# Twenty-eight transposes of the identity ahead of the first matmul of a two-layer encoder trunk

## The chip, the cores and the metric

The kernel runs on one core of one Trainium2 chip. The metric is the device time of one execution in microseconds, taken as the median of several runs; lower is better.

## What is computed

Two pre-norm residual layers over 256 tokens of width 2048, all in fp32. Layer 0 mixes tokens with bidirectional retention beside 2-D neighbourhood attention, layer 1 with differential attention; each layer then attends to 256 memory tokens and ends in a SwiGLU feed-forward of hidden width 5632.

```python
for i in range(DEPTH):                                   # DEPTH = 2
    h = rms_norm(x, norm_mix_g[i])
    if i % 2 == 0:
        x = x + retention_na_mixer(h, w_in_ab[j], ...)   # one projection: h @ w_in_ab, 2048 x 7168
    else:
        x = x + diff_attention_mixer(h, w_in_c[j], ...)
    m = rms_norm(mem, norm_mem_g[i])
    x = x + memory_cross_attention(rms_norm(x, norm_xattn_g[i]), m, ...)
    x = x + swiglu_ffn(rms_norm(x, norm_ffn_g[i]), w_ffn_in[i], w_ffn_out[i])
return x
```

## The kernel before

Nearly all of the work is large matrix products, and all of them go through one function, `gemm`. A weight matrix is cut into blocks of 512 rows by 512 columns (1 MB, tile `raw`), and each block into two units of 256 rows. `prepare` (lines 269 to 296) fetches a block with one DMA on SP's queue (line 282; the very first block comes in two halves, lines 278 and 280, with a tile of the transposed input between them) and splits each unit in two parts for accuracy: ScalarE rounds it to `wh` (line 292), and VectorE takes the remainder `wl` (line 293). Three `raw` buffers, three of `wh` and three of `wl` rotate. `gemm` calls `prepare` so that three units are ready or under way before TensorE takes one.

A unit is 12 matmuls of 128x128 by 512 columns: for each of two token halves and two row tiles, `wh` with the high part of the activations (line 321), `wl` with the high part (322), `wh` with the low part (323). So the first matmul of a unit needs `wh`, and the second needs `wl`. For the order of the first projection (list `start`, lines 245 and 246), `raw` block 0 feeds units 0 and 1, block 1 units 2 and 3, block 2 units 4 and 5, and so on; with three buffers, the DMA of block 4 (units 8 and 9) takes the buffer of block 1, and can be issued when `wl` of unit 3 has been written.

The activations come into the first projection ready transposed from DRAM (tiles `xt`, line 127), are multiplied by the gain and split into `hTh` on ScalarE (350) and `hTl` on VectorE (351). Between these lie small jobs that `Side` hands out unit by unit: the parameters, the retention decays (from line 169, a chain of small VectorE operations on tile `pl`), the lambdas, and the neighbourhood bias, whose tables come by four DMAs on POOL's queue (line 577). Every engine executes its instructions in the order in which the program issues them.

`ident`, the 128x128 identity, is made on GpSimd near the top (`make_identity`, lines 130 and 131). In the kernel before, TensorE first uses it in `turn` (line 345), where four 128x128 transposes go to one PSUM tile `pt` of the pool `ps_t`, which has two buffers. The first such call comes some way into the first projection.

Of the kernel before, what the change touches and what calls it, by code (L numbers as in the profile page):

```python
# [10 lines left out]
F32 = mybir.dt.float32  # L11
# [5 lines left out]
P = 128  # L17
D = 2048
T = 256
# [62 lines left out]
def trunk_kernel(  # L82
# [8 lines left out]
    nc = tc.nc  # L91

    def pool(name, bufs, **kw):
        return ctx.enter_context(tc.tile_pool(name=name, bufs=bufs, **kw))
# [16 lines left out]
    ps_t = pool("ps_t", 2, space=bass.MemoryType.PSUM)  # L111
# [17 lines left out]
    load_xt(0)  # L129
    ident = const.tile([P, P], F32, name="ident")  # L130
    make_identity(nc, ident)
    mhalf = const.tile([P, 16], F32, name="mhalf")
    nc.gpsimd.memset(mhalf, -0.5)
    warm = const.tile([P, 1], F32, name="warm")
# [112 lines left out]
    for layer in range(2):  # L247
        j = layer // 2
# [510 lines left out]
    for layer in range(2):  # L759
        j = layer // 2  # L760
# [150 lines left out]
```

## Time and profile before

| | us |
|---|---|
| median of 3 runs | 2475.66 |
| lowest, highest | 2475.55, 2479.15 |
| the profiled execution | 2475.84 |
| its span, first to last instruction | 2474.1 |

The profile is of one execution. It gives the busy time of each engine over the span, the chain of work that ended last, and a timeline of single instructions with the idle time ahead of each and what ended it. A matmul's listed duration includes its way through the array, and matmuls overlap; their pace is read from the distance of their starts. The granted clock of TensorE is 1.00 in every row of this profile.

### The profile page before, as it was taken

The page shows a single profiled execution, that of the slowest core. Times are in us where ns is not written, and L with a number is a line of the kernel's source. Part 1 is how long each engine was busy: PE and PEld are TensorE (multiplying, and loading weights), DVE is VectorE, ACT ScalarE, POOL GpSimd, SP SyncE. Part 2 cuts the span into 40 slices and gives each one's busy share as a digit, 9 for nine tenths or more (in the row PEclk, how much of TensorE's full clock was granted, in tenths as well). Part 3 has the DMA queues.
Part 4 walks back from the last instruction along what each step waited for, and adds up shares of the span by engine and source line. Part 5 has one row for each costly group of instructions (what it writes and reads, how often), then busy time and mean ns, then how long its engine had stood idle before and what let it go on. Part 6 is the DMA issues. An engine that isn't in the chain of part 4 may idle for free.

```text
span 2474.1 us, 28641 instructions
## 1 busy us (share of the span) xinstructions
PE 2456.3 (99%) x11184; PEld 2037.1 (82%) x11184; DVE 1475.7 (60%) x1833; ACT 1187.0 (48%) x1538; POOL 138.2 (6%) x215
## 2 busy tenths in 40 slices
PE   8999999999999999999999999999999999999999
PEld 6888888888888888888888888888888888888887
DVE  6775565675655555555567766767655545555554
ACT  6554464564443444444455555655544444443443
POOL 1000001010000000000010000010100000000000
PEclk9999999999999999999999999999999999999999
DMA  8555567656765666566674555675766656665665
GB/s 288 177 169 179 175 226 245 214 192 213 233 216 200 205 212 225 194 198 226 225 241 164 170 170 168 212 249 171 237 222 210 215 188 214 228 206 200 207 217 175
DMA packets 250184, 511.82 MB, mean 207 GB/s; under 512 B 11328, under 2 KB 11968, under 8 KB 250048
## 3 DMA queue, kind: packets, MB, share of 16 engines
q1 hardware_dynamic: 239568, 484.47, 58.5%
q0 software_dynamic: 8320, 23.08, 4.1%
q10 hardware_dynamic: 2160, 2.44, 0.3%
q8 instruction: 87, 1.43, 0.2%
q14 instruction: 49, 0.40, 0.0%
HBM read 486.88 MB, written 23.07 MB: 206 GB/s over the span
## 4 chain that ended last, share of the span: by engine, by line
PE 92%; DMA 3%; DVE 3%; ACT 1%; POOL 1%; issue 0%; ACTq 0%; SPq 0%; POOLq 0%; DVEq 0%
PE acc L322 30%; PE acc L321 30%; PE acc L323 30%; DMA zz<-zd 2%; DVE wl L293 1%; DMA zd<-zz 1%; PE pt L345 1%; ACT wh L292 0%; PE pt L545 0%; PE pa_s L437 0%; PE pa_s L436 0%; DVE x_sb L741 0%; PE pa_s L435 0%; POOL zz L394 0%; PE pa_r L595 0%
## 5 line engine op out<-in xcount | busy, mean ns | idle before, releaser
L293 DVE TENSOR_TENSOR wl<-raw,wh 128x1024 fp32r<-128x1024 f32 (+1 forms) x865 | 1053.7, 1221 | 870.8 <-ACT wh L292 870.4
L292 ACT CAST wh<-raw 128x1024 fp32r<-128x1024 f32 (+1 forms) x865 | 909.1, 1051 | 1158.2 <-PE acc L323 1132.8
L322 PE MATMUL acc<-wl,hTfh 128*128 128x512 f32 x1408 | 547.9, 389 | 0.6 <-DVE wl L293 0.6
L323 PE MATMUL acc<-wh,hTfl 128*128 128x512 f32 x1408 | 547.7, 389 | 0.0
L321 PE MATMUL acc<-wh,hTfh 128*128 128x512 f32 x1408 | 547.7, 389 | 0.0
L321 PE MATMUL acc<-wh,hTh 128*128 128x512 f32 x832 | 332.0, 399 | 9.8 <-ACT wh L292 8.3
L322 PE MATMUL acc<-wl,hTh 128*128 128x512 f32 x832 | 325.7, 391 | 0.9 <-DVE wl L293 0.9
L323 PE MATMUL acc<-wh,hTl 128*128 128x512 f32 x832 | 325.8, 392 | 0.0
L322 PEld LDWEIGHTS acc<-wl,hTfh 128*128 128x128 f32 x1408 | 264.3, 188 | 56.2 <-DVE wl L293 1.4
L323 PEld LDWEIGHTS acc<-wh,hTfl 128*128 128x128 f32 x1408 | 264.3, 188 | 54.9
L321 PEld LDWEIGHTS acc<-wh,hTfh 128*128 128x128 f32 x1408 | 264.3, 188 | 54.9
L322 PE MATMUL acc<-wl,aTh 128*128 128x512 f32 x704 | 274.0, 389 | 0.2 <-DVE wl L293 0.2
L323 PE MATMUL acc<-wh,aTl 128*128 128x512 f32 x704 | 273.9, 389 | 0.0
L321 PE MATMUL acc<-wh,aTh 128*128 128x512 f32 x704 | 273.9, 389 | 0.0
L321 PEld LDWEIGHTS acc<-wh,hTh 128*128 128x128 f32 x832 | 157.2, 189 | 40.0 <-ACT wh L292 8.3
L323 PEld LDWEIGHTS acc<-wh,hTl 128*128 128x128 f32 x832 | 156.7, 188 | 34.0
L322 PEld LDWEIGHTS acc<-wl,hTh 128*128 128x128 f32 x832 | 157.2, 189 | 31.2 <-DVE wl L293 1.8
L394 POOL DMA_DIRECT2D zz<-zd x160 | 87.3, 552 | 1589.9 <-DMA zd<-zz 1410.9
L322 PEld LDWEIGHTS acc<-wl,aTh 128*128 128x128 f32 x704 | 132.1, 188 | 28.2 <-DVE wl L293 0.8
L321 PEld LDWEIGHTS acc<-wh,aTh 128*128 128x128 f32 x704 | 132.1, 188 | 27.5
L323 PEld LDWEIGHTS acc<-wh,aTl 128*128 128x128 f32 x704 | 132.1, 188 | 27.3
L321 PE MATMUL acc<-wh,oTh 128*128 128x512 f32 x256 | 100.2, 392 | 0.0
(189 smaller groups left out, 1940.3 us busy)
## 6 DMA issues: line engine op xcount, KB each, us to landing
raw<-in_w_ffn_in SPq DMA_DIRECT2D x176, 1024.0 KB, 5.1
raw<-in_w_ffn_out SPq DMA_DIRECT2D x88, 1024.0 KB, 5.1
raw<-in_w_in_ab SPq DMA_DIRECT2D x55, 1024.0 KB, 5.2
raw<-in_w_in_c SPq DMA_DIRECT2D x48, 1024.0 KB, 5.2
zd<-zz SPq DMA_DIRECT2D x40, 512.0 KB, 3.8
zz<-zd POOLq DMA_DIRECT2D x160, 128.0 KB, 5.4
raw<-in_w_out_ab SPq DMA_DIRECT2D x16, 1024.0 KB, 5.1
raw<-in_w_xkv SPq DMA_DIRECT2D x16, 1024.0 KB, 5.0
```

Of the source, the lines that this page charges most:

```text
L292: nc.scalar.copy(wh[:, js], raw[:, rs])
L293: nc.vector.tensor_sub(wl[:, js], raw[:, rs], wh[:, js])
L321: nc.tensor.matmul(acc[t], lhsT=hi[:, kt, ts], rhs=wh[:, j], start=first and j == 0, stop=False)
L322: nc.tensor.matmul(acc[t], lhsT=hi[:, kt, ts], rhs=wl[:, j], start=False, stop=False)
L323: nc.tensor.matmul(acc[t], lhsT=lo[:, kt, ts], rhs=wh[:, j], start=False, stop=last and j == 1)
L345: nc.tensor.transpose(pt[:, j, t * P:(t + 1) * P], srcs[t][:, c:c + P], ident)
L394: nc.gpsimd.dma_start(zT[32 * j:32 * j + 32].rearrange("a (i n) -> a i n", i=4), zd[:, :, j].rearrange("i a n -> a i n"))
```

## The change

Right after the identity is made, TensorE transposes it 28 times: seven tiles named `idle` are taken in turn from the pool `ps_t` under the tag `pt`, and each gets four transposes of `ident`, laid out as in `turn`. Nothing reads these tiles. Nothing else is changed.

```diff
     load_xt(0)
     ident = const.tile([P, P], F32, name="ident")
     make_identity(nc, ident)
+
+    for _ in range(7):
+        idle = ps_t.tile([P, 2, T], F32, tag="pt", name="idle")
+        for j in range(2):
+            for t in range(2):
+                nc.tensor.transpose(idle[:, j, t * P:(t + 1) * P], ident, ident)
     mhalf = const.tile([P, 16], F32, name="mhalf")
```

## Rows read from the trace of the kernel before

**Rows 1.** The page: span, and busy time of each engine with its share.

```profile
span 2474.1 us, 28641 instructions
PE 2456.3 (99%) x11184; PEld 2037.1 (82%) x11184; DVE 1475.7 (60%) x1833; ACT 1187.0 (48%) x1538; POOL 138.2 (6%) x215
```

**Rows 2.** The page: the chain that ended last, shares by engine.

```profile
PE 92%; DMA 3%; DVE 3%; ACT 1%; POOL 1%; issue 0%; ACTq 0%; SPq 0%; POOLq 0%; DVEq 0%
```

**Rows 3.** TensorE's waits, 0 to 200 us: total, times, longest.

```profile
PE acc L321 <- ACT wh L292: 8.3, 1, 8.3
PE pa_o L436 <- DVE pl L430: 1.6, 1, 1.6
...
```

**Rows 4.** Timeline of TensorE: start, duration, instruction, idle before it and its releaser.

```profile
8.28 0.80 PE L321 MATMUL acc<-wh,hTh 128*128 128x512 f32 x1 [8.28 <-ACT wh L292]
9.49 0.80 PE L322 MATMUL acc<-wl,hTh 128*128 128x512 f32 x1 [0.42 <-DVE wl L293]
10.08 0.63 PE L323 MATMUL acc<-wh,hTl 128*128 128x512 f32 x1
...
13.92 0.56 PE L323 MATMUL acc<-wh,hTl 128*128 128x512 f32 x1
14.32 0.39 PE L321 MATMUL acc<-wh,hTh 128*128 128x512 f32 x1
14.54 0.39 PE L322 MATMUL acc<-wl,hTh 128*128 128x512 f32 x1
...
33.36 0.40 PE L321 MATMUL acc<-wh,hTh 128*128 128x512 f32 x1
33.59 0.40 PE L322 MATMUL acc<-wl,hTh 128*128 128x512 f32 x1
...
97.97 0.40 PE L321 MATMUL acc<-wh,hTh 128*128 128x512 f32 x1
98.20 0.40 PE L322 MATMUL acc<-wl,hTh 128*128 128x512 f32 x1
```

**Rows 5.** Timeline of VectorE: the remainders wl of units 0 to 6 and 8.

```profile
8.74 1.29 DVE L293 TENSOR_TENSOR wl<-raw,wh 128x512 fp32r<-128x512 f32 x2
...
11.54 1.22 DVE L293 TENSOR_TENSOR wl<-raw,wh 128x1024 fp32r<-128x1024 f32 x1
...
15.07 2.35 DVE L293 TENSOR_TENSOR wl<-raw,wh 128x1024 fp32r<-128x1024 f32 x2
...
20.04 2.36 DVE L293 TENSOR_TENSOR wl<-raw,wh 128x1024 fp32r<-128x1024 f32 x2
23.76 1.22 DVE L293 TENSOR_TENSOR wl<-raw,wh 128x1024 fp32r<-128x1024 f32 x1 [1.37 <-ACT wh L292]
...
32.10 1.22 DVE L293 TENSOR_TENSOR wl<-raw,wh 128x1024 fp32r<-128x1024 f32 x1 [1.23 <-ACT wh L292]
```

**Rows 6.** Timeline of ScalarE: wh of units 3 and 8.

```profile
14.52 1.05 ACT L292 CAST wh<-raw 128x1024 fp32r<-128x1024 f32 x1 [0.83 <-DVE pl L187]
...
31.01 1.05 ACT L292 CAST wh<-raw 128x1024 fp32r<-128x1024 f32 x1 [3.35 <-DMA raw<-in_w_in_ab]
```

**Rows 7.** Timelines of SP (block 4 issued) and POOL (identity made, bias tables issued).

```profile
17.45 0.38 SPq L282 DMA_DIRECT2D raw<-in_w_in_ab  x1
...
1.57 0.28 POOL masks.py:199 TENSOR_SCALAR_AFFINE_SELECT ident<-ident 128x128 f32<-128x128 f32 x1
...
16.71 2.62 POOL L577 DMA_DIRECT2D bias<-in_na_rpb  x4 [0.37 <-POOL bias L572]
```

**Rows 8.** Stretches: length, busy time by engine, granted clock, DMA share, GB/s.

```profile
8.00:20.00 12.00, 11.31 (x38) 8.79 (x39) 10.74 (x35) 7.51 (x14) 2.82 (x5) 1.00 1.04 391
20.00:28.00 8.00, 8.00 (x37) 6.64 (x36) 5.53 (x7) 6.08 (x11) 0.00 (x0) 1.00 1.05 242
28.00:46.00 18.00, 18.00 (x81) 14.89 (x80) 12.60 (x18) 11.93 (x21) 0.00 (x0) 1.00 1.03 373
```

**Rows 9.** Timeline of TensorE: six transposes in a row, later in the kernel.

```profile
530.47 0.82 PE L345 MATMUL pt<-ident,x_sb 128*128 128x128 f32 x6
```

## The prediction, made before the change was run

> **What bounds the kernel now.** I read the page first. TensorE is busy for 99% of the span [rows 1] and makes up 92% of the chain that ended last [rows 2], so time saved elsewhere is worth nothing, and a matmul that starts earlier is worth something only if no later supply makes TensorE wait again. Next I read TensorE's waits [rows 3]: the longest is the one at the start, 8.3 us until the first weights have landed and been rounded. The change works inside that wait. Its own first matmuls stand in the timeline of TensorE [rows 4]. The first starts at 8.28, the second waits for `wl` until 9.49, and from 10.08 to 13.92 ten matmuls start over nine equal steps: (13.92 - 10.08) / 9 = 0.427 us. From 14.32 on the steps are shorter: from 14.32 to 33.36 lie seven units of 12, so (33.36 - 14.32) / 84 = 0.227 us. 512 columns in 0.427 us are 1.2 GHz, the lower level of the clock; 0.227 us belongs to the upper one. The granted clock reads 1.00 in the stretch of 8 to 20 us as in the others [rows 8], so that column does not show the difference here, and I go by the pace. Before the pace rose at 14.32, TensorE had been idle up to 8.28 and had then done one unit.
>
> **The prize, if all of it arrives.** At the upper level from the second matmul on, unit 0 ends its issue at 9.49 + 11 x 0.227 = 11.99 instead of 14.32 [rows 4]. That is 2.33 us, and the largest gain that the early clock can give, since from 14.32 on the pace is the upper one already.
>
> **The transposes themselves.** They need only the identity, done at 1.57 + 0.28 = 1.85 [rows 7]; I let them start at 2.0. Later in the kernel six transposes in a row take 0.82 us [rows 9], and one alone 0.27 of that, so the step is about (0.82 - 0.27) / 5 = 0.11 us. That is at the upper level. No row shows transposes at the lower one. Lower bound: 0.11 us each, 3.1 us for 28, done at 5.1. My value is 0.11 times the ratio of the matmul's two paces, 0.427 / 0.227 = 1.88: 0.207 us each, 5.8 us, done at 7.8, which is 0.5 us before the first matmul. Upper bound: no faster than the 512-column matmul at the lower level, 0.427 us each, 12.0 us, done at 14.0. I take the middle value because the transpose has a row of its own and only the clock is scaled. TensorE is the only engine that gets new instructions; no queue of SP, ScalarE or POOL is passed, and no DMA is added. Queued behind them on TensorE is the first matmul alone. The second cannot start before 9.49 anyway, so the cover is 28 transposes ending by about 9.1, and beyond that each late microsecond delays unit 0. The two buffers of `ps_t` are taken over within the seven tiles without a reader, so no other engine is waited for; if each of the five take-overs drained the array, that would be 5 x 0.27 = 1.4 us more and an end at 9.2, still about inside the cover. Below nothing this cannot go. The next user of those buffers comes tens of microseconds later.
>
> **Where the 2.33 us go.** Now I follow units 1 to 8 with the new start and the old supply. That supply doesn't follow TensorE. VectorE works from 8.74 to 22.40 on remainders, low parts of activations and the chain of decays; its pieces of that stretch [rows 5] have no idle time before them that TensorE ended. So the `wl` times stand as they are:
>
> - Unit 1 could begin at 11.99, but its `wl` is done at 11.54 + 1.22 = 12.76. Its second matmul goes then instead of at 12.22: a stall of about 0.6 us, and unit 2 begins at 12.8 + 11 x 0.227 = 15.3.
> - Unit 2: `wl` done at the middle of the pair, 15.07 + 2.35 / 2 = 16.25. Stall of 0.7 to 0.8 us; unit 3 begins at 18.8 instead of 19.76.
> - Units 3 to 7: `wl` of unit 3 is done at 17.42, of units 4 and 5 by 22.40, before they are wanted, so unit 8 would begin at 18.8 + 5 x 2.72 = 32.4 instead of 33.36. ScalarE gets back the `wh` buffers sooner, so that units 6 and 7 are no later than before relative to TensorE.
> - Unit 8: its `wh` started at 31.01 after 3.35 us of waiting for the DMA [rows 6], and its `wl` is done at 32.10 + 1.22 = 33.32 [rows 5]. Before, its second matmul went at 33.59 [rows 4]. That is a margin of 0.27 us, and this margin is all that can be gained as long as the block's landing doesn't move.
>
> Does the landing move? The block's DMA was issued at 17.45 [rows 7], just after the remainder of unit 3 freed the buffer at 17.42 [rows 5], and that is in VectorE's unmoved stretch. From then to its landing the DMA engines are full: share 1.04 to 1.05 in the rows from 8 to 28 us, and 1.03 after [rows 8]. What can be issued earlier are the bias tables at 16.71 [rows 7]. ScalarE rounds unit 3 at 14.52 [rows 6]; the page puts the 0.83 us before it down to a `pl` that it does not read, and I take it for the wait for unit 0's `wh` buffer, which unit 0's last matmul, begun at 13.92 [rows 4], gives back. At most 0.83 us of that would be gained for the gains behind it and for the tables. But they share the same full engines and landed ahead of block 4 before as well, so the bytes in front of block 4 are the same. I cost that at nothing; bounds are 0.8 us earlier or later at unit 8.
>
> So 2.33 - 0.6 - 0.75 - 0.77 = 0.21 us are left, which agrees with the margin of 0.27 less a handover of some 0.06 us from `wl` to the matmul (8.74 plus a little over half of 1.29 against 9.49 [rows 4, 5] puts that at up to 0.1). Behind unit 8 the chain is mostly TensorE's, and its other waits end on work that TensorE itself released, so 0.2 us reach the end. The longest of these idle times, 1.6 us [rows 3], did not bring the slow pace back: at 97.97 and 98.20 the step is 0.23 [rows 4]. So the pause between the last transpose and 9.49, about as long at 0.207 us each, should not either, though there the transposes stand in the place of matmuls.
>
> **The sum.** The profiled execution is 2475.84 = 2474.1 of span and 1.7 around it. With 0.2 less it is 2475.6. The median is 0.2 below the profiled execution, so the forecast for the median is 2475.66 - 0.2 = 2475.5.
>
> **The rivals.**
>
> 1. The change doesn't do what it says: the pace stays at 0.427 us until 14.3 because the transposes don't lift the clock. Nothing in the trace shows a stretch of transposes by themselves, so no row decides it. The transposes end at 7.8, in the cover, and the time is that of before: 2475.7. The Trainium skill has this as a rule, in "TensorE: Matmul & The Clock Gate", Part 4: PE-mode transpose: the upper level is said not to engage for transposes, since they do not count as TensorE's work in the same way. By that rule this change gives nothing; no run shown here tests it.
> 2. The weights come sooner too: block 4 lands earlier by what the early clock moves ahead of it. With the 0.8 us of the bound above it is 2475.5 - 0.8 = 2474.7; if no later block binds either, the full gain, 2475.66 - 2.33 = 2473.3. Against it speaks the full DMA [rows 8].
> 3. Slower: the transposes run past the cover. The place is the second matmul at 9.49. If the clock does not rise, it decides from (9.49 - 2.0) / 28 = 0.27 us for each; at the upper bound of 0.427 they end at 14.0, unit 0 is 14.0 - 9.5 = 4.5 us late, and the time is 2480.1. If the clock has risen by the end of them, the stalls above absorb 2.1 us first, it decides from (9.49 + 2.33 - 2.0) / 28 = 0.35 us, and at 14.0 the loss is 4.5 - 2.3 = 2.2 us: 2477.8. Against it: the rows of transposes put 0.207 us well below both points.
>
> **How the numbers follow.** The forecast has a chance of 0.54, rival 1 of 0.30, rival 2 of 0.07, rival 3 of 0.09. They differ by little: 2475.5, 2475.7, 2473.3 to 2474.7, 2477.8 to 2480.1. A measurement of this kernel can tell about 0.2% from no change, which is 5 us here. The largest possible gain is 2.33 us, under half of that; rival 3 reaches 4.5 us at its worst. So faster has 0.02 and slower 0.03, for what I have not seen, and no change has 0.95. The range goes from the full gain, 2473.3, to the mild end of rival 3, 2477.8, and leaves out the worst of it; the three runs of before lie within 2475.55 to 2479.15, so a single run can be above.
>
> **What would show it.** In the profile after: transposes of `ident` from about 2.0, step near 0.2 us, ended before 8.28. For the forecast, steps of 0.227 us right behind 9.49, and three new waits of line 322 for `wl`, near 12.2, 15.5 and 32.6, of 0.6, 0.75 and 0.8 us; unit 8's second matmul near 33.4, and all later work 0.2 us early. Steps of 0.427 up to about 14.3 would be rival 1. A first or second matmul later than 9.49 would be rival 3. A `wh` of unit 8 that starts well before 31.0 would be rival 2. I would be wrong altogether if the end moved by more than 2.4 us down or 4.5 up.

## The result, and the profile after

| | before | after |
|---|---|---|
| median, both in one comparison | 2476.60 us | 2479.81 us |
| lowest, highest | 2474.20, 2480.47 | 2477.86, 2483.92 |
| the profiled execution, its span | 2475.84, 2474.1 | 2481.13, 2479.4 |

The ratio after to before is 1.0014, with a 95% interval of 1.0007 to 1.0020: 1.7 to 5.0 us slower, 3.2 us between the medians. The forecast was 0.2 us faster, with a range that ended at 2477.8.

The page after, against [rows 1, 2]: TensorE is busy 3.1 us longer, and its share of the chain rises from 92 to 94%.

```profile
span 2479.4 us, 28696 instructions
PE 2459.4 (99%) x11212; PEld 2040.8 (82%) x11212; DVE 1476.1 (60%) x1833; ACT 1187.0 (48%) x1538; POOL 138.5 (6%) x215
...
PE 94%; DVE 2%; DMA 2%; ACT 0%; POOL 0%; issue 0%; ACTq 0%; SPq 0%; DVEq 0%; POOLq 0%
```

The timeline of TensorE, against [rows 4] (all lines of the kernel are six higher than before, so 327, 328 and 329 are the three matmul lines):

```profile
8.29 0.79 PE L327 MATMUL acc<-wh,hTh 128*128 128x512 f32 x1 [8.29 <-ACT wh L298]
...
11.81 0.63 PE L327 MATMUL acc<-wh,hTh 128*128 128x512 f32 x1
12.24 4.14 PE L137 MATMUL idle<-ident 128*128 128x128 f32 x28
16.13 0.48 PE L328 MATMUL acc<-wl,hTh 128*128 128x512 f32 x1
...
17.37 0.40 PE L327 MATMUL acc<-wh,hTh 128*128 128x512 f32 x1
```

This one view overthrows the premise of the forecast. The first 8.29 us of TensorE are as empty as before. The 28 transposes stand at 12.24, behind the seventh matmul of unit 0, in the middle of the work that they were to precede. They hold TensorE for 16.13 - 12.24 = 3.89 us. The five matmuls behind them then take 17.37 - 16.13 = 1.24 us instead of 14.32 - 12.24 = 2.08, since the pace rose while the transposes ran. So unit 1 starts at 17.37 instead of 14.32: 3.89 - 0.84 = 3.05 us late.

The place is no accident of the execution: the program has them there as built. An engine runs its instructions in the order of the built program, and the build does not keep the order of the source. On ScalarE the built order over the opening changed as well, and VectorE's remainders follow it; SP's and POOL's did not:

```
before:  wh 1, 2, 3 | hTh 4 to 7 | wh 4, 5 | ... | wh 6 | hTh 8 | wh 7 | hTh 9 to 11 | wh 8
after:   wh 1, 2 | hTh 4 to 7 | wh 3, 4 | ... | wh 5 | hTh 8 to 10 | wh 6 | hTh 11 | wh 7
```

(the number behind `wh` is the unit, the one behind `hTh` the row tile of the activations). ScalarE's timeline before has, behind `wh` of unit 3 [rows 6], these lines:

```profile
15.47 1.71 ACT L350 ACTIVATE hTh<-xt,gcol 128x256 fp32r<-128x256 f32 x4
...
23.63 0.51 ACT L350 ACTIVATE hTh<-xt,gcol 128x256 fp32r<-128x256 f32 x1
25.40 1.05 ACT L292 CAST wh<-raw 128x1024 fp32r<-128x1024 f32 x1 [1.26 <-PE acc L323]
26.35 1.31 ACT L350 ACTIVATE hTh<-xt,gcol 128x256 fp32r<-128x256 f32 x3
```

In ScalarE's timeline after, the changed order has a price of its own: three `hTh` wait for a tile of transposed input until 27.15, and `wh` of unit 6 stands behind them.

```profile
12.68 1.04 ACT L298 CAST wh<-raw 128x1024 fp32r<-128x1024 f32 x1 [1.66 <-DMA raw<-in_w_in_ab]
13.63 1.70 ACT L356 ACTIVATE hTh<-xt,gcol 128x256 fp32r<-128x256 f32 x4
17.57 1.05 ACT L298 CAST wh<-raw 128x1024 fp32r<-128x1024 f32 x1 [2.24 <-PE acc L329]
...
27.15 1.31 ACT L356 ACTIVATE hTh<-xt,gcol 128x256 fp32r<-128x256 f32 x3 [3.07 <-DMA xt<-in_x_t]
28.36 1.04 ACT L298 CAST wh<-raw 128x1024 fp32r<-128x1024 f32 x1
```

So there are two suspects: the place of the transposes on TensorE, and the new order on the other engines. Of the 3.05 us, 0.9 come back where TensorE waited 1.6 us before [rows 3]; its wait there is 0.7 after:

```profile
PE pa_o L442 <- DVE pl L436: 0.7, 1, 0.7
```

Followed matmul by matmul, this profile is behind that wait between 1.5 and 2.7 us late up to 1600 us. The rest of the 5.3 us between the two spans arises between 1600 and 1900 us, in waits of this execution (3.4 us there against 0.8 before); a second profile of the changed kernel ends 2.5 us above the span of before.

### The profile page after: what moved, and what is told of

Read it like the earlier page. It is cut to its first block, busy times and chain, and to the rows that moved or that the text cites. A ratio compares the mean times of both kernels' runs of the same rounds, so it can differ in the third digit from the quotient of the medians.

```text
span 2479.4 us, 28696 instructions
## 1 busy us (share of the span) xinstructions
PE 2459.4 (99%) x11212; PEld 2040.8 (82%) x11212; DVE 1476.1 (60%) x1833; ACT 1187.0 (48%) x1538; POOL 138.5 (6%) x215
## 4 chain that ended last, share of the span: by engine, by line
PE 94%; DVE 2%; DMA 2%; ACT 0%; POOL 0%; issue 0%; ACTq 0%; SPq 0%; DVEq 0%; POOLq 0%
PE acc L328 30%; PE acc L327 30%; PE acc L329 30%; DMA zz<-zd 1%; PE pt L351 1%; DVE wl L299 1%; DMA zd<-zz 0%; PE pt L551 0%; PE pa_s L443 0%; PE pa_s L442 0%; PE pa_s L441 0%; PE pa_r L601 0%; ACT wh L298 0%; DVE x_sb L747 0%; DMA lrow<-in_lambda_k 0%
## 5 line engine op out<-in xcount | busy, mean ns | idle before, releaser
L328 PEld LDWEIGHTS acc<-wl,aTh 128*128 128x128 f32 x704 | 132.2, 188 | 27.5
```

The lines of the kernel that those rows point to most:

```text
L328: nc.tensor.matmul(acc[t], lhsT=hi[:, kt, ts], rhs=wl[:, j], start=False, stop=False)
```

## The experiments

**Is it the length of what stands between the matmuls?** One tile of transposes instead of seven, and fourteen:

```diff
-    for _ in range(7):
+    for _ in range(1):      # few4;  range(14) in many56
```

> The change with one tile instead of seven: 4 transposes, which stand in the built order at the same place, after the seventh matmul of unit 0. Theory A (place and length): 4 steps of 0.213 us push unit 0's last five matmuls back by 0.85 us, some of it given back because the pace rises at about 14.3 as before; unit 1 starts near 14.8 instead of 14.32, and the time is 2476.6 to 2477.1 us. Theory B (the order on the other engines, changed by the mere presence of transposes, costs the 3 us): 2479 to 2480 us.

> The change with fourteen tiles instead of seven: 56 transposes after the seventh matmul of unit 0. Theory A (length on the path): the added 28 run at the upper pace, 0.11 us each, so 3.1 us more than the changed kernel: unit 1 starts near 20.4 instead of 17.37, and the time is about 2482.9 us. Theory B (one-off disturbance): 2479.8 us as with 28.

few4: 1.0002 [0.9993, 1.0011], medians 2475.30 against 2475.20. many56: 1.0026 [1.0016, 1.0035], 2482.18 against 2475.20, 7.0 us. TensorE's timelines, few4 first, then many56:

```profile
12.08 0.60 PE L137 MATMUL idle<-ident 128*128 128x128 f32 x4
...
13.68 0.39 PE L327 MATMUL acc<-wh,hTh 128*128 128x512 f32 x1
```

```profile
12.29 7.04 PE L137 MATMUL idle<-ident 128*128 128x128 f32 x56
...
20.33 0.39 PE L327 MATMUL acc<-wh,hTh 128*128 128x512 f32 x1
```

With 56, unit 1 starts at 20.33, 2.96 us behind the changed kernel: 28 more at 0.11 us. So the length counts, but many56 is not a clean test of it: its ScalarE, VectorE and SP stand in a further changed order, and by unit 9 short delays have made the 2.96 us 3.6. Its 7.0 us are 3.8 more than the changed kernel's 3.2, and the intervals are about 2 us either way. With four, unit 1 even starts early (13.68), because the pace rose sooner in that execution; and few4's built order is nearly that of before, so it clears neither suspect.

**The transposes where the words put them.** The matmuls of the first units get an edge, an ordering that the build has to keep, which puts them behind the last transpose:

```diff
+                    if at["phase"] == 1 and b < 2 and u < 2:
+                        tc.add_manual_dep(head.ins, last_idle.ins.name, ...NoSync..., reason="idle first")
```

> The same 28 transposes, but the matmuls of the first units carry an edge that puts them behind the last transpose in TensorE's order; nothing else is edited. Theory A (place): the change cost time only because the built program has the transposes after the seventh matmul of unit 0, at 12.24 us. Then here they run from about 2.0 to 8 us at steps of 0.21 us or less, nothing of them is on the path, and the time is that of before or up to 1 us less: 2475.6 to 2476.6 us against 2476.6. If transposes alone lift the clock, the steps behind 9.5 us are 0.227 us, else 0.427 us up to about 14.3; the time tells these two apart by 0.2 us at most, the timeline does. Theory B (count): 28 transposes ahead of or inside the opening cost their 3 us wherever they stand, or disturb the order of the other engines by as much: 2479.8 us as in the changed kernel.

> 56 transposes with the edge that puts them ahead of the first matmul. If transposes alone lift the clock, their step falls from 0.21 to 0.11 us within the row, they end between 9 and 12 us, and the stalls for wl that the prediction reckoned (2.1 us in all) take up the lateness: the time is within 0.5 us of before, 2476.1 to 2477.1 us. If they don't lift it, they run at 0.21 us to the end, 2.0 + 56 x 0.21 = 13.8 us, unit 0 is 4.3 us late and the time is up to 2481 us.

Both missed by far: early28 1.0036 [1.0023, 1.0048], 2484.65 against 2475.20; early56 1.0046 [1.0034, 1.0059], 2486.79. The timeline of TensorE in early28 (331 and 332 are the second and third matmul lines), then its stretches (length, busy time and count by engine, granted clock, DMA share, GB/s):

```profile
1.91 4.72 PE L137 MATMUL idle<-ident 128*128 128x128 f32 x28 [1.91 <-POOL ident masks.py:199]
8.48 0.50 PE L327 MATMUL acc<-wh,hTh 128*128 128x512 f32 x1 [1.84 <-ACT wh L298]
9.83 0.51 PE L331 MATMUL acc<-wl,hTh 128*128 128x512 f32 x1 [0.85 <-DVE wl L299]
10.17 0.40 PE L332 MATMUL acc<-wh,hTl 128*128 128x512 f32 x1
...
29.84 0.79 PE L327 MATMUL acc<-wh,hTh 128*128 128x512 f32 x1 [3.81 <-ACT wh L298]
31.16 0.79 PE L331 MATMUL acc<-wl,hTh 128*128 128x512 f32 x1 [0.53 <-DVE wl L299]
```

```profile
2.00:4.00 2.00, 2.00 (x10) 2.00 (x11) 0.00 (x0) 0.68 (x2) 0.89 (x4) 1.00 0.81 237
4.00:6.00 2.00, 2.00 (x16) 2.00 (x15) 1.25 (x6) 0.91 (x2) 0.00 (x0) 1.00 0.54 168
...
32.00:34.00 2.00, 2.00 (x6) 1.52 (x6) 1.84 (x3) 1.05 (x3) 0.00 (x0) 0.50 0.80 212
```

The opening is what the forecast wanted: the transposes start at 1.91, the count per 2 us rises from 10 to 16 while nothing but transposes runs, and from 10.17 the matmuls step at 0.23 us. Unit 1 starts 1.83 us early, at 12.49. Then it is lost: at unit 5 TensorE idles 3.81 us for a `wh`, the granted clock falls to 0.50, and the twelve matmuls of the unit run at the slow pace. ScalarE's timeline names the cause, the one seen in the changed kernel, now one unit earlier: `wh` of unit 5 stands behind three `hTh` whose input lands at 27.5.

```profile
27.54 1.31 ACT L359 ACTIVATE hTh<-xt,gcol 128x256 fp32r<-128x256 f32 x3 [6.72 <-DMA xt<-in_x_t]
28.76 1.03 ACT L298 CAST wh<-raw 128x1024 fp32r<-128x1024 f32 x1
```

The edge had rearranged the other engines further. In early56 it is VectorE's order: in unit 3 TensorE waits 8.94 us for a `wl` that stands behind a `bias`, whose table lands near 28.4 us. A first try to mend the order kept only the `hTh` and `hTl` behind the `wh` and `wl` of before:

```diff
+AFTER = {4: 3, 5: 3, 6: 3, 7: 3, 8: 6, 9: 7, 10: 7, 11: 7, 12: 10, ...}   # row tile: unit
...
+            if (gi, layer) == (0, 0) and k in AFTER:
+                behind(ins, AFTER[k])
```

> The 28 transposes ahead of the first matmul as in early28, with twelve more ordering edges that keep each hTh and hTl of the later row tiles behind the wh and wl that they stood behind in the kernel before. If the 9 us of early28 were ScalarE's order (hTh of row tiles 8 to 10 ahead of wh of unit 5, waiting for their input until 27.5 us), the loss is gone: unit 6 starts within 1 us of 27.9 and the time is within 1 us of before. If the early transposes themselves cost the 9 us, the time stays near 2484.

early28L: 1.0037 [1.0025, 1.0049], 2483.95 against 2475.50; a miss. The squares of `x_sb` (line 338 of before) now stood ahead of `wh` of unit 7, and TensorE idled 5.51 us there.

**Place and order apart.** Two kernels take one suspect each. early4 is early28 with one tile of transposes: they take 1.1 us inside the first wait, and ScalarE, VectorE, SP and POOL have exactly the built order of the changed kernel. lockmid28 is the changed kernel with edges that chain the first 60 instructions of ScalarE and 110 of VectorE in the order of before; all four engines then stand as before, and the transposes stay inside unit 0.

```diff
+    for engine, order in ORDER_BEFORE.items():
+        for a, b in zip(order, order[1:]):
+            tc.add_manual_dep(traced[engine][b], traced[engine][a].name, ...NoSync..., reason="order of before")
```

> Four transposes with the edge that puts them ahead of the first matmul. They take under 1 us inside the wait for the weights, so TensorE loses nothing to them directly; but the built order of ScalarE, VectorE, SP and POOL over the opening is, instruction for instruction, that of the changed kernel. Theory place (the changed kernel lost its 3 us to the transposes between the matmuls of unit 0): the time is that of before within 1 us. Theory order (it lost them to the new order of the other engines, four hTh ahead of wh of unit 3 and three hTh ahead of wh of unit 6): unit 6 waits for wh behind a transposed input that lands at about 27 us, TensorE stalls there by 1.5 to 3 us, and the time is 1.5 to 3 us above before. Both may hold in part, since transposes that have made TensorE 3 us late hide such a stall.

> The changed kernel with added ordering edges that give ScalarE and VectorE, over the opening, the order that they have in the kernel before; SP and POOL have it anyway. The 28 transposes stay after the seventh matmul of unit 0. What is left of the change is the place on TensorE. Theory place: unit 1 starts 3.05 us late, 0.9 us at most are given back at the wait of 1.6 us near 97 us, and the time is 2 to 3 us above before. Theory order (the loss comes from the new order of the other engines alone): within 0.5 us of before.

> The changed kernel once more, beside lockmid28 and lockearly28 on one chip: 3.2 us above before as measured, between 1.7 and 5.0. If place and order each cost and the two add, it lies above lockmid28 by the cost of the order alone; if the later of the two decides, it equals the larger of lockmid28 and early4.

| ratio to before [95%] | other engines as before | other engines as in the change |
|---|---|---|
| nothing between the matmuls | 1 (before) | 1.0018 [1.0009, 1.0026] (early4) |
| 28 transposes inside unit 0 | 1.0013 [1.0004, 1.0022] (lockmid28) | 1.0014 [1.0007, 1.0020], again 1.0018 [1.0009, 1.0027] (the change) |

Either alone is enough, and together they cost no more than one, as far as intervals of some 2 us either way can tell. TensorE in early4, with ScalarE's line that releases it, then TensorE in lockmid28 (330 and 331 are the first and second matmul lines):

```profile
29.56 0.51 PE L327 MATMUL acc<-wh,hTh 128*128 128x512 f32 x1 [1.62 <-ACT wh L298]
30.88 0.50 PE L331 MATMUL acc<-wl,hTh 128*128 128x512 f32 x1 [0.82 <-DVE wl L299]
...
27.27 1.31 ACT L359 ACTIVATE hTh<-xt,gcol 128x256 fp32r<-128x256 f32 x3 [6.67 <-DMA xt<-in_x_t]
28.48 1.03 ACT L298 CAST wh<-raw 128x1024 fp32r<-128x1024 f32 x1
```

```profile
12.54 4.34 PE L140 MATMUL idle<-ident 128*128 128x128 f32 x28
16.64 0.48 PE L331 MATMUL acc<-wl,hTh 128*128 128x512 f32 x1
...
17.87 0.39 PE L330 MATMUL acc<-wh,hTh 128*128 128x512 f32 x1
```

In early4 TensorE comes to unit 6 on time, finds no `wh`, and idles 1.62 + 0.82 us. In the changed kernel ScalarE waits for the same input until 27.15, but TensorE is 3.05 us late by then and asks for unit 6 just as it is ready: its timeline there shows no idle time. One lateness hides in the other, though not always whole: in the second profile of the changed kernel TensorE waits 0.25 us in unit 6 and 0.21 in unit 8, and unit 9 starts 3.98 us late, against 3.03 in the first, 3.52 in lockmid28 and 2.84 in early4.

early4 costs more than its expected 1.5 to 3 us: 4.5 by the ratio, 5.8 between the medians (2481.34 against 2475.50). Nine of its 11 executions have a mean granted clock below 1.000; the profiled one, 2479.71, has not. What the others lost beyond the stall shown is not in its trace.

**The change as meant, with everything else held.** In early28z the build itself puts the work first: 28 fp32r matmuls of the same shape on a tile of ones that VectorE fills. All other engines keep the order of before. lockearly28 is early28 with the locks (ScalarE, VectorE and SP), lockearly48 the same with 48 transposes.

```diff
+    still = const.tile([P, P], F32, name="still")
+    nc.vector.memset(still, 1.0)
-                nc.tensor.transpose(idle[:, j, t * P:(t + 1) * P], ident, ident)
+                nc.tensor.matmul(idle[...], lhsT=still.bitcast(F32R), rhs=still.bitcast(F32R), start=True, stop=True)
```

> 28 fp32r matmuls of 128x128 by 128 on a tile of ones that VectorE fills at the start stand in for the transposes of the identity. The build then puts them ahead of the first weight matmul, and ScalarE, SP, POOL and VectorE (but for the fill) keep the order of the kernel before. The prediction's theory: they run from 1 to 2 us on, the pace is 0.227 us from the second weight matmul on, TensorE stalls for wl in units 1, 2 and 8 (0.6, 0.75 and 0.8 us), unit 8's second matmul goes near 33.4, and the time is 0.2 us below before, no change that can be measured. Rival (an early clock by itself upsets the opening, which is why the early transposes lost 9 us): unit 5 or 6 starts several us late and the time is 4 to 9 us above before.

> The change as its words have it: 28 transposes of the identity ahead of the first matmul, and all other engines locked to the order of the kernel before. The prediction's sum: within 0.5 us of before (0.2 us below it), whether the clock is up at 9.5 us or not; if it is up, unit 1 starts near 12.0 and TensorE stalls in units 1, 2 and 8. Rival (early transposes cost 8 to 9 us as in early28 and early28L, whatever the order): 2484.

> As lockearly28 with 48 transposes, so that they last until about the time at which the second weight matmul can go and leave no pause in which the clock could fall. They end between 7 us (if the step falls to 0.11 us early) and 12 us. The prediction's supply sum: unit 0 runs at 0.227 us, the stalls in units 1, 2 and 8 take up what is early or late, unit 8's second matmul goes within 1 us of 33.6, and the time is within 0.7 us of before. Rival (the early clock alone is worth its full 2.33 us): 2.3 us below before.

early28z 1.0003 [0.9994, 1.0011]; lockearly28 1.0008 [1.0000, 1.0017]; lockearly48 1.0000 [0.9991, 1.0009]. The 9 us are gone, and lockearly28 differs from early28 by the locks alone. Nothing is won either: at best no change, in lockearly28 perhaps 2 us lost where at most 0.5 was expected, at the edge of its interval. In early28z the pace did not rise early (it was slow until 12.9 us), so it shows only that such work inside the first wait costs nothing. The early clock itself is seen in lockearly28, whose profiled execution, 2474.93, is its fastest, and in lockearly48. The timeline of TensorE in lockearly28 (330, 334, 335 are the matmul lines) can be laid beside the prediction's list:

```profile
1.91 5.54 PE L140 MATMUL idle<-ident 128*128 128x128 f32 x28 [1.91 <-POOL ident masks.py:199]
8.03 0.50 PE L330 MATMUL acc<-wh,hTh 128*128 128x512 f32 x1 [0.58 <-ACT wh L301]
9.45 0.50 PE L334 MATMUL acc<-wl,hTh 128*128 128x512 f32 x1 [0.92 <-DVE wl L302]
...
12.07 0.39 PE L330 MATMUL acc<-wh,hTh 128*128 128x512 f32 x1
12.77 0.50 PE L334 MATMUL acc<-wl,hTh 128*128 128x512 f32 x1 [0.31 <-DVE wl L302]
...
15.42 0.39 PE L330 MATMUL acc<-wh,hTh 128*128 128x512 f32 x1
16.30 0.50 PE L334 MATMUL acc<-wl,hTh 128*128 128x512 f32 x1 [0.49 <-DVE wl L302]
...
33.02 0.50 PE L330 MATMUL acc<-wh,hTh 128*128 128x512 f32 x1 [0.29 <-ACT wh L301]
34.28 0.50 PE L334 MATMUL acc<-wl,hTh 128*128 128x512 f32 x1 [0.76 <-DVE wl L302]
```

Unit 1 starts 2.25 us early, unit 2 1.62, unit 3 0.79, and at unit 8 nothing is left.

## Why the prediction was wrong, point by point

- **"I let them start at 2.0": the step that failed.** The sum put the transposes where the source has them. The build put them at 12.24, on the path, and unit 1 started 3.05 us late. All three rivals shared that premise, the slow one too: it made the transposes run past the cover, never start outside it. That 2479.81 lies in its span of 2477.8 to 2480.1 is chance. What the transposes cost was priced well: the starts of single transposes lie 0.213 and 0.109 us apart at the two paces, against the 0.207 and 0.11 of the sum; 28 at either alone would be 6.0 and 3.1 us, and the measured 3.89 us lies between, since the pace rose among them.
- **The rows could have told.** [Rows 7] shows the second half of `ident` at 1.57. In POOL's timeline before, the lines below, the first half stands at 0.74, and between them lie `mhalf` and `tdiff`, which the source has later. And the decays, one run of lines in the source, are split up by `wl` and `hTl` in VectorE's timeline, from which [rows 5] shows only the `wl`. Both say that source order is not built order. I wrote the opposite into the description of the kernel.

```profile
0.74 0.20 POOL masks.py:197 MEMSET ident<- 128x128 f32 x1 [0.29 <-POOLq L890]
0.89 0.11 POOL L133 MEMSET mhalf<- 128x16 f32 x1
1.03 0.56 POOL L137 IOTA tdiff<- 128x512 f32 x1
```

- **"TensorE is the only engine that gets new instructions; no queue of SP, ScalarE or POOL is passed": true, and misleading.** No other engine got an instruction, but ScalarE and VectorE got another order, so the `wl` times did not "stand as they are". early4 shows that this order alone costs 1.0018 [1.0009, 1.0026].
- **The clock.** Right in its main point: transposes alone lift it. In early28 the count per 2 us goes from 10 to 16 with transposes alone on TensorE. The Trainium skill says in "TensorE: Matmul & The Clock Gate", Part 4: PE-mode transpose, that the upper level does not engage for transposes; the rows of early28 disagree, and the measurement decides (the trace lists these transposes as MATMUL and does not name a mode). Rival 1 falls as a rule. As a chance it stands: in early28z, with matmuls of that shape, the pace stayed slow until 12.9.
- **The pause behind the last transpose.** "Should not" bring the slow pace back was too sure. In lockearly28 the pace held over a pause from 7.45 to 9.45 with one matmul in it. In early28L, with the same transposes and much the same pause (7.43 to 9.75), it fell; its stretches, columns as above:

```profile
8.00:10.00 2.00, 0.74 (x2) 0.43 (x3) 1.10 (x3) 1.71 (x5) 0.00 (x0) 0.99 1.02 396
10.00:12.00 2.00, 2.00 (x6) 1.50 (x6) 1.93 (x9) 1.04 (x1) 0.00 (x0) 0.50 1.05 397
```

- **Where the 2.33 us go: right, once the order is held.** Predicted for unit 1: start 11.99, second matmul near 12.8; lockearly28 has 12.07 and 12.77. Unit 2: 15.3 and a stall of 0.75; 15.42, and a second matmul 0.88 behind the first, a stall of 0.65. Unit 8 is the limit, as said. Only its landing was not as fixed as I held: `wh` of unit 8 starts at 31.92 in lockearly28, 32.03 in early28z and 32.08 in lockearly48 against 31.01 before [rows 6], so the second matmul goes at 34.28, 0.69 us later than before. This lies inside the bound of 0.8 us that I had given. In those three, the block after next is issued 0.3 to 0.8 us earlier (26.95 to 27.44 against 27.74), into a full queue. few4 speaks against this as the cause: there it is issued at 27.10, and `wh` of unit 8 starts at 31.16. What delays block 4 in the three stays open.
- **The landing of block 4 was held to be fixed by the full DMA engines: it can move.** In the kernel before, the bias tables are issued from 16.71 on, block 4 at 17.45 [rows 7], and it lands 13.5 us later. In lockmid28, where all comes later, block 4 is issued at 20.41, the tables behind it from 20.75 on, and it lands after 5.1 us, at 25.5: over 5 us sooner than before, from an issue 3 us later. That the tables make the difference is not shown, and early transposes with the tables held behind block 4 were not tried. The lines are POOL's in lockmid28, then the blocks issued from 16 to 23 us with their size and the median time to landing, lockmid28 first:

```profile
20.75 2.62 POOL L586 DMA_DIRECT2D bias<-in_na_rpb  x4 [0.31 <-POOL bias L581]
...
raw<-in_w_in_ab SPq DMA_DIRECT2D x1, 1024.0 KB, 5.1
...
raw<-in_w_in_ab SPq DMA_DIRECT2D x2, 1024.0 KB, 13.5
```

- **"Its other waits end on work that TensorE itself released":** 0.9 of the 3.05 us were taken back at the wait of 1.6 us [rows 3], which I had let pass whole.

What stays open: why the clock rose at 4.9 us in early28, 6.5 us in lockearly28 and not before 12.9 in early28z, each seen in one execution; and by what rule the build chose the place, of which the runs show only that matmuls on a tile filled by VectorE came first and transposes of the identity from POOL behind seven matmuls.

## What to carry to other kernels

Work that is to fill an idle stretch must be seen there in the built order, on its own engine and on all others, before it is priced; where a scheduler orders the program, source order is a wish. The trace of before already tells whether it is kept: look for one run of source lines that stands split or swapped in a timeline. And an early start is worth what the supply allows: 2.3 us of faster matmuls here were worth nothing, because a block of weights came no sooner. Ask then whether that block can be made to land sooner: here it took 13.5 us with the bias tables issued from 0.7 us ahead of it, and 5.1 us with them behind it.

## What the runs showed of the hardware

A stall can cost twice. Idle for 3.81 us at unit 5, TensorE came back at the slow pace in early28, and its twelve matmuls took 6.0 us with their waits (29.84 to 35.85) instead of 2.7. The idle time of 1.6 us [rows 3] did no such thing. It happens in the middle of the kernel too: lockearly48 was profiled in an execution of 2481.76 us, 6.9 above its median of 2474.89, and a line of its timeline and a stretch show where most of it went.

```profile
1272.40 0.79 PE L334 MATMUL acc<-wl,hTh 128*128 128x512 f32 x1 [3.10 <-DVE wl L302]
```

```profile
1274.00:1278.00 4.00, 4.00 (x12) 3.09 (x11) 0.91 (x2) 0.51 (x1) 3.50 (x5) 0.54 0.84 271
```

Here a wait of 3.10 us is followed by matmuls at a granted clock near 0.5 until 1277.7; ahead of it TensorE is 0.3 us behind the kernel before, and after it 5.7. In the profile of before no wait in that place is longer than 0.5 us. Four of the changed kernel's 22 executions have a mean granted clock of 0.999 instead of 1.000; they took 2481.6 to 2483.9 us, all above the median, and fit the same picture, but no trace of them shows it.
